# Gating the S5 output by halves of the tokens, and keeping its first half on chip until the output projection

## The chip, the cores and the metric

The kernel runs on one core of a Trainium2 chip. A core has TensorE for matrix products (PE in the profile; PEld is its weight load), VectorE (DVE), ScalarE (ACT), GpSimd (POOL), and SyncE (SP), which here issues nearly all transfers between HBM and the on-chip SBUF. The engines run their own instruction lists in order and wait for each other by semaphores. PSUM is the memory that TensorE writes its results to; it has eight banks of 2 KB per partition.

The metric is the time on the device in microseconds, as the median of several executions. One more execution is recorded by the profiler; the trace is from that one.

## What is computed

One layer of a hybrid decoder with 1024 tokens of width 1024 in float32: an input projection feeds eight RWKV heads (512 channels) and an S5 state-space group (512 channels); what both give is joined, projected by `w_out`, gated and added to the residual; then comes a SwiGLU feed-forward part (FFN). Cut to what matters here:

```python
def rwkv7_time_mix(...):          # sequential in the tokens; done here by chunks
    ...                           # S <- S*w + (S a) b + v k ;  y = S r
    y = (y - mu) * lax.rsqrt(var + LNX_EPS) * lnx_w + lnx_b
    y = y + jnp.sum(r_h * k_h * r_k, axis=-1, keepdims=True) * v_h
    return y.reshape(bsz, seq, D_RWKV) * g

def s5_mix(...):
    ...                           # y: (B, T, 512), out of the state-space recurrence
    zz = jax.nn.gelu(y)
    out = zz * jax.nn.sigmoid(zz @ w_glu + b_glu)
    return rms_norm(out) * gain

ada = c_act @ w_ada[l] + b_ada[l]                 # six vectors of 1024
sh_m, sc_m, g_m, sh_f, sc_f, g_f = jnp.split(ada, 6, axis=-1)
mix = jnp.concatenate([y_rwkv, y_s5], axis=-1) @ w_out[l]
x = x + g_m[:, None, :] * mix
h = modulate(rms_norm(x), sh_f, sc_f)
ffn = (jax.nn.silu(h @ ffn_w_gate[l]) * (h @ ffn_w_up[l])) @ ffn_w_down[l]
x = x + g_f[:, None, :] * ffn
```

## The kernel before

**Products.** A float32 product is three passes with operands split into a rounded part and a remainder: `split(dst, src, eng)` lets ACT cast the rounded part (L131 of the helper) and `eng` subtract it (`lo_part`, L127). So every operand of a split product costs one ACT and one POOL or DVE instruction ahead of TensorE.

**Stages.** After the S5 part, RWKV goes by four quarters of 256 tokens, `qt` 0 to 3. Each has `prepare` and `post` (matrices of the chunks, a triangular solve on DVE in which `XU`, `stmp` and `LU` take part, a trip through DRAM in `x_d`), `chains` (four chunks in sequence, each of four steps with products into `p` and small DVE copies `R`, `U`, `ST` between them) and `finishes` (`finish(q)` for two groups of four heads: norm, gate, `ld` written to `y_d`). Two other strands run beside quarter 1: `s5_glu`, the gate of S5's output, and `ada_steps`, which makes three of the six adaLN vectors (48 loads `wada` of 256 KB, four per step, in four buffers; of twelve steps, half accumulate `acc` wholly on DVE at L297, and half by ACT, L299, and POOL, L300). Then `outproj(0)` projects the first 512 tokens (`po`), and the first half's FFN runs while RWKV's quarters 2 and 3 are woven into it. `outproj(1)` and the second half's FFN end the program.

**s5_glu.** S5's output lies in DRAM (`z_d`) by position within chunks of eight tokens: `z_d[t]` holds position t of all 128 chunks. The GLU takes four units of 256 tokens; unit `hf` is positions 2hf and 2hf+1 of all chunks, so a unit holds tokens of the whole sequence. Per unit: two loads `zz`, a split of it (`zhl`), four products `pglu` of 12 matmuls into the PSUM banks `s` and `p` in turn, `sg`/`zz` (L807, L808), the sum of squares on POOL, one product `pss` into bank `s`, the scale `ra`, `rs` (L819, L820), four scalings of `zz` on DVE (L823) and one write to rows 512 to 1023 of `y_d` (L825).

**outproj(half).** For each half of the output columns (`dh`) it goes over k = 4, 5, 6, 7, 0, 1, 2, 3, eight pieces of 128 rows of `w_out`; k of 4 and above are S5's. Per k it loads `yt` from `y_d` (in the first `dh`), splits it into `yhl`, loads `wraw`, splits that into `wo` (POOL does the remainder), and issues 12 matmuls `po` into four banks. These banks have the tags `s`, `p`, `A` and `G` and are also those of RWKV, the GLU and adaLN. A half has 192 `po` in all.

**What sets the order.** The code is emitted by generators that `weave` interleaves with given weights; then a scheduler with modelled times of its own fixes each engine's instruction list. In the stage of the chains of quarter 0 (`c0`) the call is `weave(c0, (LIM(glg, 18), 2), LIM(adg, 12))`: up to 18 steps of the GLU and 12 of adaLN beside them.

Of the kernel before, what the change touches and what calls it, by code (L numbers as in the profile page):

```python
# [29 lines left out]
def kernel(  # L30
# [745 lines left out]
    def s5_glu(glp):  # L776
# [21 lines left out]
        nxt = load(0)
        for hf in range(4):
            zz, hl = nxt  # L800
            ssum = glp.tile([P, 256], F32, tag="x2", bufs=6, name="ssum")
            for m in range(4):
# [485 lines left out]
    def outproj(half, xp, op, tags, gp, gt):  # L1288
# [18 lines left out]
        for dh in range(2):  # L1307
            sl = slice(HT * dh, HT * dh + HT)
            pss = [ps_t(t, "po") for t in tags]
            for k in order:  # L1310
# [22 lines left out]
    def norm_f(half, xp, tags):  # L1333
# [158 lines left out]
```

## Time and profile before

| what | value |
| --- | --- |
| median of 3 runs | 1584.49 us (1580.01 to 1585.1) |
| the profiled execution | 1576.36 us |
| its span in the trace | 1574.6 us |
| mean granted TensorE clock | 0.937 |
| TensorE busy | 1418.4 us, 90% of the span |
| VectorE, ScalarE, GpSimd busy | 925.9, 574.6 and 553.4 us |

All trace numbers are from the profiled execution, which is 8.1 us faster than the median of the runs. Its time is 1.8 us more than its span. The stretch that the change touches lies between 425 and 725 us: the chains of quarter 0 with GLU and adaLN, the chains and finishes of quarter 1, the first half's output projection and the first FFN block. The granted clock is 1.00 where TensorE runs at the upper of its two levels (2.4 GHz) all the time; at 0.5 it is at 1.2 GHz.

### The profile page before, as it was taken

What the parts mean: (1) busy time and instruction counts of PE and PEld (TensorE: products, weight loads), DVE (VectorE), ACT (ScalarE), POOL (GpSimd) and SP (SyncE); (2) the same over time, 40 slices, a digit from 0 to 9 for tenths busy, and PEclk for the clock granted to TensorE, in tenths of its full rate; (3) what the DMA queues carried; (4) which work ended last, traced back from release to release, by engine and by line L of the source; (5) the groups of instructions that cost most, each with busy time, mean ns of one, the idle gap of its engine ahead of it and who ended that gap; (6) DMA issues with size and microseconds to landing.
All of it is one profiled execution on the core that took longest, in us unless ns stands there. A gap on an engine that the chain in (4) does not pass through costs nothing.

```text
span 1574.6 us, 22988 instructions
## 1 busy us (share of the span) xinstructions
PE 1418.4 (90%) x9071; PEld 1145.1 (73%) x9071; DVE 925.9 (59%) x1591; ACT 574.6 (36%) x924; POOL 553.4 (35%) x499
## 2 busy tenths in 40 slices
PE   3897798898968868898999998999997999999997
PEld 3776586776757647776777786778886888888885
DVE  6977328889687964854478654547347433433335
ACT  4432334554345554242154222224333322222223
POOL 4359435332164425381000026001511254544443
PEclk9889898999889758999999998999998999999999
DMA  9724555353456444254042344216422333232331
GB/s 291 228 97 140 167 173 165 108 153 102 91 160 175 140 132 140 68 128 94 28 121 81 101 101 94 81 55 199 143 74 77 124 101 100 91 97 94 107 94 54
DMA packets 259885, 187.67 MB, mean 119 GB/s; under 512 B 71479, under 2 KB 228801, under 8 KB 259777
## 3 DMA queue, kind: packets, MB, share of 16 engines
q1 hardware_dynamic: 256048, 178.00, 38.5%
q10 hardware_dynamic: 2912, 7.64, 1.4%
q8 instruction: 71, 1.16, 0.3%
q0 software_dynamic: 816, 0.57, 0.2%
q14 instruction: 38, 0.30, 0.1%
HBM read 157.11 MB, written 31.16 MB: 120 GB/s over the span
## 4 chain that ended last, share of the span: by engine, by line
PE 58%; DVE 16%; DMA 8%; POOL 8%; ACT 4%; issue 4%; SPq 1%; ACTq 0%; DVEq 0%; POOLq 0%
PE pdn L270 12%; PE pgate L270 12%; PE pup L270 12%; PE pz L270 6%; PE po L1320 3%; PE p L1065 2%; POOL stmp L1009 2%; POOL XU L1011 2%; DVE acc L297 2%; PE pu L367 2%; PE pY L765 1%; DMA wada<-in_w_ada_dram 1%; DMA XU<-x_d 1%; PE pA L965 1%; DMA raw_g<-in_ffn_w_gate_dram 1%
## 5 line engine op out<-in xcount | busy, mean ns | idle before, releaser
L270 PE MATMUL pdn<-wd,act 128*128 128x512 f32 x1056 | 271.8, 398 | 1.0 <-DVE x L1369 0.8
L270 PE MATMUL pup<-h,hl_up 128*128 128x512 f32 x1056 | 264.9, 394 | 0.2 <-ACT hl_up L131 0.2
L270 PE MATMUL pgate<-h,hl_g 128*128 128x512 f32 x1056 | 262.5, 394 | 2.0 <-ACT hl_g L131 1.9
L270 PEld LDWEIGHTS pdn<-wd,act 128*128 128x128 f32 x1056 | 197.3, 190 | 48.5 <-issue 2.5
L270 PEld LDWEIGHTS pgate<-h,hl_g 128*128 128x128 f32 x1056 | 196.5, 188 | 46.8 <-issue 2.9
L270 PEld LDWEIGHTS pup<-h,hl_up 128*128 128x128 f32 x1056 | 197.1, 188 | 43.8 <-issue 2.1
L1369 DVE TENSOR_TENSOR x<-pdn,x 128x512 f32<-128x512 f32 x176 | 118.8, 687 | 183.7 <-PE pdn L270 183.5
L270 PE MATMUL pz<-hT,hl_z 128*128 128x256 f32 (+1 forms) x912 | 185.8, 361 | 27.3 <-ACT zo L875 8.4
L270 PEld LDWEIGHTS pz<-hT,hl_z 128*128 128x128 f32 x912 | 151.3, 206 | 57.5 <-ACT zo L875 11.8
L1404 DVE TENSOR_TENSOR rawd<-rawd,gfb 128x1024 f32<-128x1024 f32 x44 | 56.9, 1294 | 98.0 <-DMA rawd<-in_ffn_w_down_dram 76.9
L1320 PE MATMUL po<-wo,yhl 128*128 128x512 f32 x384 | 94.7, 398 | 1.4 <-POOL wo L127 0.8
L131 ACT CAST hl_up<-raw_up 128x1024 fp32r<-128x1024 f32 x44 | 46.2, 1051 | 118.7 <-PE pup L270 105.7
L131 ACT CAST wd<-rawd 128x1024 fp32r<-128x1024 f32 x44 | 45.6, 1051 | 118.7 <-DVE rawd L1404 84.6
L1320 PEld LDWEIGHTS po<-wo,yhl 128*128 128x128 f32 x384 | 72.3, 190 | 18.5 <-POOL wo L127 1.7
L127 POOL TENSOR_TENSOR hl_g<-raw_g,hl_g 128x1024 fp32r<-128x1024 f32 x19 | 45.6, 2398 | 80.1 <-ACT hl_g L131 76.1
L127 POOL TENSOR_TENSOR yhl<-yt,yhl 128x512 fp32r<-128x512 f32 x16 | 23.2, 1457 | 143.5 <-ACT yhl L1305 140.1
L1398 ACT ACTIVATE sgt<-pgate 128x512 f32<-128x512 f32 x44 | 26.3, 599 | 120.7 <-PE pgate L270 120.5
L1009 POOL TENSOR_TENSOR stmp<-LU,XU 128x126 f32<-128x126 f32 (+22 forms) x62 | 31.6, 510 | 108.9 <-DMA LU<-l_d 104.2
L127 POOL TENSOR_TENSOR wd<-rawd,wd 128x1024 fp32r<-128x1024 f32 x19 | 49.8, 2619 | 55.4 <-ACT wd L131 55.4
L878 POOL TENSOR_TENSOR zo<-zo,zm 128x512 f32<-128x512 f32 x28 | 43.9, 1568 | 70.3 <-ACT zo L875 58.3
L127 POOL TENSOR_TENSOR wo<-wraw,wo 128x512 fp32r<-128x512 f32 x32 | 43.0, 1350 | 72.8 <-ACT wo L131 72.8
L127 POOL TENSOR_TENSOR hl_up<-raw_up,hl_up 128x1024 fp32r<-128x1024 f32 x19 | 49.7, 2617 | 50.7 <-ACT hl_up L131 50.7
(373 smaller groups left out, 2461.5 us busy)
## 6 DMA issues: line engine op xcount, KB each, us to landing
raw_g<-in_ffn_w_gate_dram SPq DMA_DIRECT2D x44, 512.0 KB, 3.9
raw_up<-in_ffn_w_up_dram SPq DMA_DIRECT2D x44, 512.0 KB, 3.8
rawd<-in_ffn_w_down_dram SPq DMA_DIRECT2D x44, 512.0 KB, 3.3
wada<-in_w_ada_dram SPq DMA_DIRECT2D x24, 512.0 KB, 8.3
raw_z<-in_w_in_dram SPq DMA_DIRECT2D x24, 512.0 KB, 5.5
wada<-in_w_ada_dram SPq DMA_DIRECT2D x48, 256.0 KB, 3.5
wraw<-in_w_out_dram SPq DMA_DIRECT2D x32, 256.0 KB, 3.3
zt_d<-zo SPq DMA_DIRECT2D x28, 256.0 KB, 2.8
```

The lines of the kernel that those rows point to most:

```text
L127: (eng or G).tensor_tensor(out=out, in0=a, in1=b, op=ALU.subtract)
L131: S.copy(dst[:, 0], src)
L270: PE.matmul(ps, lhsT=lf(a, k), rhs=rf(b, k), start=(n == 0), stop=(n == 3 * kb - 1))
L297: V.scalar_tensor_tensor(out=acc, in0=wt, scalar=cact[:, k:k + 1], in1=acc, op0=ALU.mult, op1=ALU.add)
L367: PE.matmul(pu[hf, b], lhsT=uw[b][:, a_, k, :], rhs=hT[hf, k][:, b_, :], start=(k == 0 and n == 0), stop=(k == 7 and n == 2))
L878: G.tensor_tensor(out=o, in0=o, in1=zm[:, 0:HT], op=ALU.add)
L1009: SOLVE.tensor_tensor(out=t, in0=LU[:, j, j + 1:32].unsqueeze(2).to_broadcast([P, nt, nk]), in1=X[:, j:j + 1, 0:nk].to_broadcast([P, nt, n ...
L1011: SOLVE.tensor_tensor(out=X[:, j + 1:32, 0:nk], in0=X[:, j + 1:32, 0:nk], in1=t, op=ALU.add)
L1065: PE.matmul(ps[r, h], lhsT=a, rhs=b, start=(n == 0), stop=(n == len(ops) - 1))
L1320: PE.matmul(pss[i], lhsT=yh[k][:, a, 128 * i:128 * i + 128], rhs=wo[:, b], start=(k == 4 and n == 0), stop=(k == 3 and n == 2))
L1369: V.tensor_tensor(out=t, in0=ps, in1=t, op=ALU.add)
L1404: V.tensor_tensor(out=raw, in0=raw, in1=gfb, op=ALU.mult)
```

## The change

A GLU unit is now four of the eight positions, but only of the first or second 64 chunks: units 0 and 1 hold the first 512 tokens, units 2 and 3 the rest. A load of `zz` is four transfers with runs of 256 bytes in place of two with 512. The first half's y is not written to DRAM. It is split (ACT copy, POOL remainder) straight into `yh[4]` to `yh[7]`, which take the SBUF slots of the first quarter's matrices `ak0` and `ak1`. The second half's y still goes to `y_d`, in eight writes instead of two. `finish` of quarter 1 splits its `ld` on DVE into the second half of `yh[0]` to `yh[3]` and writes no `y_d`; of quarter 0 it writes as before, and `outproj(0)` loads only those 256 tokens.

The weave of the chains of quarter 0 takes four steps of the GLU (the first unit's products) and no more, so the other units come with quarter 1. `wraw` has three buffers, and in half 0 the remainder of `wo` is made by DVE for odd k, by POOL for even k.

```diff
-        def load(hf):
+        def load(u):
             zz = glp.tile([P, 4, 256], F32, tag="zz", bufs=2, name="zz")
-            for t in range(2):
-                nc.sync.dma_start(zz[:, :, 128 * t:128 * t + 128], z_d[2 * hf + t].rearrange("b c g j -> (c g) b j"))
+            half, t0 = u // 2, 4 * (u % 2)
+            for t in range(4):
+                nc.sync.dma_start(zz[:, :, 64 * t:64 * t + 64],
+                                  z_d[t0 + t, :, :, :, 64 * half:64 * half + 64].rearrange("b c g j -> (c g) b j"))
...
+            if u == 0:
+
+                for q in range(2):
+                    t = RP[0].tile([P, 2, 2, HT], F32R, tag=f"ak{q}", name="y5")
+                    for x in range(2):
+                        yh[4 + 2 * q + x] = t[:, x]
             for m in range(4):
                 V.scalar_tensor_tensor(out=zz[:, m], in0=zz[:, m], scalar=hga[:, m:m + 1], in1=rs,
                                        op0=ALU.mult, op1=ALU.mult)
-            nc.sync.dma_start(y_d[512:1024, 256 * hf:256 * hf + 256].rearrange("(m p) t -> p m t", p=P), zz)
+                if half == 0:
+                    v = zz[:, m].rearrange("p (t j) -> p j t", t=4)
+                    d = yh[4 + m].rearrange("p x (j t) -> p x j t", t=8)[:, :, :, t0:t0 + 4]
+                    S.copy(d[:, 0], v)
+                    lo_part(d[:, 1], v, d[:, 0], G)
+                else:
+                    nc.sync.dma_start(
+                        y_d[512 + 128 * m:640 + 128 * m, :].rearrange("p (t j) -> p t j", t=8)[:, t0:t0 + 4, 64:128],
+                        zz[:, m].rearrange("p (t j) -> p t j", t=4))
...
         V.tensor_tensor(out=d, in0=pg, in1=rs, op=ALU.mult)
-        nc.sync.dma_start(y_d[256 * q:256 * q + 256, QT * qt:QT * qt + QT].rearrange("(h p) t -> p h t", h=2),
-                          d.rearrange("p (h t) -> p h t", h=2))
+        if qt == 1:
+            for h in range(2):
+                split(yh[2 * q + h][:, :, QT:HT], d[:, QT * h:QT * h + QT], V)
...
-    weave(c0, (LIM(glg, 18), 2), LIM(adg, 12))
+    weave(c0, LIM(glg, 4), LIM(adg, 12))
...
         def y_load(k):
+            if half == 0 and k >= 4:
+                return
+            n = HT if half else QT
...
-                raw = op.tile([P, HT], F32, tag="wraw", bufs=2, name="wraw")
+                raw = op.tile([P, HT], F32, tag="wraw", bufs=3, name="wraw")
...
-                split(wo, raw, G)
+                split(wo, raw, (V if k % 2 else G) if half == 0 else G)
```

Three places in the engines' lists show how the order moves. Before, SyncE's list behind the last load of quarter 1's solve (`VT<-x_d`) reads as follows; `wada` are the loads of `ada_steps`, `zz<-z_d` those of a GLU unit, `y_d<-zz` the write of one:

```order
L1024 DMA VT<-x_d 64x16x32 x2
L825 DMA y_d<-zz 128x4x256
L285 DMA wada<-in_w_ada_dram 128x2x256
L793 DMA zz<-z_d 128x4x128 x2
L285 DMA wada<-in_w_ada_dram 128x2x256 x7
L825 DMA y_d<-zz 128x4x256
L285 DMA wada<-in_w_ada_dram 128x2x256 x3
L793 DMA zz<-z_d 128x4x128 x2
L285 DMA wada<-in_w_ada_dram 128x2x256 x9
```

And in the changed kernel, from the same load on:

```order
L1040 DMA XU<-x_d 128x16x16 x2
L1041 DMA VT<-x_d 64x16x32 x2
L285 DMA wada<-in_w_ada_dram 128x2x256 x32
L902 DMA kz<-zt_d 128x2x256
L794 DMA zz<-z_d 128x4x64 x4
L1341 DMA wraw<-in_w_out_dram 128x1x512
L902 DMA rz<-zt_d 128x2x256
L1341 DMA wraw<-in_w_out_dram 128x1x512
L1147 DMA y_d<-ld 128x2x256
L1341 DMA wraw<-in_w_out_dram 128x1x512
```

The 32 loads that come here up to the end of adaLN are the same; GLU loads and writes that stood among them are gone from the row or stand behind it.

On TensorE, the end of quarter 1 before: `pd`, `pv`, `pg` are the three products of a `finish`, `pw` and `pa` belong to quarter 2's `prepare`, `pss` to the last GLU unit, and this is where the first `po` stands:

```order
L1102 MATMUL pd<-ar,cen 128x512
L904 MATMUL pw<-wzk,wa_132 128x256 x2
L816 MATMUL pss<-ssum,ones 128x256
L1102 MATMUL pd<-ar,cen 128x512
L904 MATMUL pa<-wzk,wa_132 128x256 x2
L1109 MATMUL pv<-lsq,blk 128x512 x2
L1124 MATMUL pg<-gs,g2w 128x256 x4
L1270 MATMUL pgb<-dgb,ones 128x128 x2
L1320 MATMUL po<-wo,yhl 128x512 x8
```

The same place in the changed kernel, from quarter 2's last `pa` on (18 more `po` stand ahead of these rows; `y_4563` and `y_4564` are the kept S5 rows):

```order
L921 MATMUL pa<-wzk,wa_132 128x256 x2
L1346 MATMUL po<-wo,y_4563 128x512 x6
L1346 MATMUL po<-wo,y_4564 128x512 x3
L1119 MATMUL pd<-ar,cen 128x512
L819 MATMUL pss<-ssum,ones 128x256
L1119 MATMUL pd<-ar,cen 128x512
L1346 MATMUL po<-wo,y_4563 128x512 x6
L1346 MATMUL po<-wo,y_4564 128x512 x3
L1126 MATMUL pv<-lsq,blk 128x512
L1346 MATMUL po<-wo,y_4564 128x512 x12
L1126 MATMUL pv<-lsq,blk 128x512
L1346 MATMUL po<-wo,yhl 128x512 x10
```

60 of the 192 `po` of half 0 now stand ahead of the last `pg`, against none, and 132 behind it.

On VectorE, the rows around the first GLU scaling `ra<-pss` before, right behind the solve's last instruction (`VT<-XU`):

```order
L1074 COPY U<-p_4521 128x128
L1012 COPY VT<-XU 128x32x16
L819 TENSOR_SCALAR ra<-pss 128x256
L1078 TENSOR_TENSOR ST<-p_4588,ST 128x128
L252 TENSOR_TENSOR ra<-ra,rs 128x256
L1079 TENSOR_TENSOR ST<-ST,pc 128x128
L253 SCALAR_TENSOR_TENSOR ra<-ra,rs 128x256
L254 SCALAR_TENSOR_TENSOR rs<-ra,rs 128x256
L823 SCALAR_TENSOR_TENSOR zz<-zz,hga,rs 128x256 x4
```

And the rows around unit 0's `ra<-pss` in the changed kernel, where `acc` are adaLN's accumulations and `lsq`, `lrs` belong to a `finish` of quarter 0:

```order
L307 SCALAR_TENSOR_TENSOR mod<-pac_4522,cols 128x2
L297 SCALAR_TENSOR_TENSOR acc<-wada,cact,acc 128x256
L1091 COPY U<-p_4592 128x128
L252 TENSOR_TENSOR lsq<-lsq,lrs 128x512
L297 SCALAR_TENSOR_TENSOR acc<-wada,cact,acc 128x256
L253 SCALAR_TENSOR_TENSOR lsq<-lsq,lrs 128x512
L297 SCALAR_TENSOR_TENSOR acc<-wada,cact,acc 128x256
L254 SCALAR_TENSOR_TENSOR lrs<-lsq,lrs 128x512
L822 TENSOR_SCALAR ra<-pss 128x256
L1134 SCALAR_TENSOR_TENSOR lrs<-ld,cols,lrs 128x256 x2
L1135 SCALAR_TENSOR_TENSOR lrs<-lrs,cols,bo 128x256
```

All of adaLN's accumulations on VectorE now stand ahead of the first GLU scaling; before, the first three GLU scalings stood among them.

## Rows read from the trace of the kernel before

**Rows 1.** The windows view, by the stages of this stretch (us from the span's start): chains of quarter 0 with the solve of quarter 1; chains of quarter 1; finishes of quarter 1; output projection of half 0; first FFN preparation. Busy time (instructions) of each engine, granted clock, DMA share, GB/s.

```profile
core 0: us, PE busy (x) PEld busy (x) DVE busy (x) ACT busy (x) POOL busy (x), PEclk, DMA share, GB/s
425.00:476.60 51.60, 38.56 (x545) 33.23 (x546) 41.77 (x110) 24.73 (x60) 27.52 (x38) 0.74 0.55 150
476.60:567.50 90.90, 74.59 (x989) 61.97 (x987) 75.33 (x175) 45.48 (x96) 37.19 (x43) 0.80 0.55 161
567.50:595.00 27.50, 16.21 (x32) 7.28 (x32) 17.82 (x36) 16.70 (x27) 3.76 (x3) 0.62 0.49 152
595.00:646.00 51.00, 49.37 (x210) 39.15 (x210) 25.47 (x34) 19.72 (x33) 28.87 (x22) 0.96 0.32 98
646.00:674.30 28.30, 22.13 (x221) 17.86 (x219) 24.02 (x46) 11.30 (x23) 9.46 (x6) 1.00 0.35 82
```

**Rows 2.** The chain of waits that ends last, through 500 to 597 us: start us, duration us, what.

```profile
503.89 3.89 DMA wada<-in_w_ada_dram
508.58 3.26 DMA wada<-in_w_ada_dram
...
548.23 2.71 DMA wada<-in_w_ada_dram
...
582.33 1.68 DVE zz L823 x4
584.02 3.25 DMA y_d<-zz
587.29 7.23 DMA yt<-y_d
594.56 1.10 issue
595.70 1.54 POOL yhl L127
```

**Rows 3.** The timeline: the last instruction of `finish(1)` of quarter 1, the end of half 0's last `po` and what TensorE does next (start us, duration us).

```profile
594.20 0.69 DVE L1125 TENSOR_TENSOR ld<-pg,lrs 128x512 f32<-128x512 f32 x1
...
641.74 5.10 PE L1320 MATMUL po<-wo,yhl 128*128 128x512 f32 x20
646.77 0.44 PE L965 MATMUL pA<-ar,bk 64*64 64x128 f32 x4
```

**Rows 4.** The chain of waits again, inside `outproj(0)`: 36 `po` in a row without a gap.

```profile
632.96 8.46 PE po L1320 x36
```

**Rows 5.** Groups by line and shape from 435 to 600 us: count, busy us, mean ns of one, idle time before them and what ended it.

```profile
L300 POOL TENSOR_TENSOR acc<-acc,wada 128x256 f32<-128x256 f32 x42 | 34.1, 812 | 24.2 <-DVE U L1074 11.0 <-PE pn L924 5.5 <-ACT wada L299 5.5
...
L297 DVE SCALAR_TENSOR_TENSOR acc<-wada,cact,acc 128x256 f32<-128x256 f32 x42 | 22.8, 544 | 0.2
...
L823 DVE SCALAR_TENSOR_TENSOR zz<-zz,hga,rs 128x256 f32<-128x256 f32 x16 | 8.6, 598 | 0.1
...
L808 DVE SCALAR_TENSOR_TENSOR zz<-sg,zz 128x256 f32<-128x256 f32 x16 | 8.3, 516 | 5.7 <-ACT sg L807 5.7
...
L1078 DVE TENSOR_TENSOR ST<-p,ST 128x128 f32<-128x128 f32 x16 | 4.5, 283 | 0.3
...
L127 POOL TENSOR_TENSOR wo<-wraw,wo 128x512 fp32r<-128x512 f32 x3 | 3.8, 1268 | 17.6 <-ACT wo L131 17.6
...
L1125 DVE TENSOR_TENSOR ld<-pg,lrs 128x512 f32<-128x512 f32 x4 | 2.7, 682 | 0.1
...
L1305 ACT CAST yhl<-yt 128x512 fp32r<-128x512 f32 x2 | 2.1, 1079 | 0.2 <-DMA yt<-y_d 0.2
...
L1140 DVE TENSOR_SCALAR gs<-gs 128x256 f32<-128x256 f32 x2 | 0.9, 450 | 0.0
```

**Rows 6.** The groups of the tile `act`, VectorE's line of them: remainders of 128x512 made by VectorE (min, median, max ns).

```profile
L127 DVE TENSOR_TENSOR act<-sgt,act x44: 678/787/1706, 688.9 to 1553.0; 128x512 fp32r<-128x512 f32 x44
```

**Rows 7.** The timeline of SyncE's queue: issue runs of `wada` loads (duration is that of the whole run), and the loads of `VT`.

```profile
436.03 2.04 SPq L285 DMA_DIRECT2D wada<-in_w_ada_dram  x4
...
480.58 1.87 SPq L1024 DMA_DIRECT2D VT<-x_d  x2
...
488.34 13.39 SPq L285 DMA_DIRECT2D wada<-in_w_ada_dram  x7
...
508.58 18.54 SPq L285 DMA_DIRECT2D wada<-in_w_ada_dram  x9
...
545.72 12.00 SPq L285 DMA_DIRECT2D wada<-in_w_ada_dram  x7
```

**Rows 8.** The view of transfers, groups of two tiles: KB each, median us from issue to landing.

```profile
wada<-in_w_ada_dram SPq DMA_DIRECT2D x48, 256.0 KB, 3.5
...
zz<-z_d SPq DMA_DIRECT2D x8, 256.0 KB, 3.1
```

**Rows 9.** The groups of the tile `wada` from 425 to 575 us: `acc` at L295 (min, median, max ns).

```profile
L295 DVE TENSOR_SCALAR acc<-wada,cact x12: 336/353/2456, 441.7 to 555.6; 128x256 f32<-128x256 f32 x12
```

**Rows 10.** The timeline around the longest of those, both of its neighbours on POOL and DVE (start us, duration us).

```profile
448.91 2.41 POOL L127 TENSOR_TENSOR zhl<-zz,zhl 128x1024 fp32r<-128x1024 f32 x1
449.01 2.46 DVE L295 TENSOR_SCALAR acc<-wada,cact 128x256 f32<-128x256 f32 x1
```

**Rows 11.** The timeline behind the projection: quarter 2's `LU` loads on SyncE, the first FFN product, and the first solve product of quarter 2 with its wait in brackets.

```profile
671.20 1.79 SPq L1001 DMA_DIRECT2D LU<-l_d  x2
...
674.27 0.96 PE L270 MATMUL pgate<-h,hl_g 128*128 128x512 f32 x3
...
720.53 1.92 PE L1031 MATMUL pG<-XU,ak 32*32 32x32 f32 x64 [4.59 <-DMA XU<-x_d]
```

More of the change, by code (lines that the diff above doesn't have):

```diff
@@ L798, in s5_glu @@
         nxt = load(0)
-        for hf in range(4):
+        for u in range(4):
+            half, t0 = u // 2, 4 * (u % 2)
             zz, hl = nxt
@@ L811, in s5_glu @@
                     G.tensor_tensor(out=ssum, in0=ssum, in1=sg, op=ALU.add)
-                if m == 2 and hf < 3:
-                    nxt = load(hf + 1)
+                if m == 2 and u < 3:
+                    nxt = load(u + 1)
                 yield
@@ L1125, in finish @@
         V.tensor_tensor(out=d, in0=pg, in1=rs, op=ALU.mult)
-        nc.sync.dma_start(y_d[256 * q:256 * q + 256, QT * qt:QT * qt + QT].rearrange("(h p) t -> p h t", h=2),
-                          d.rearrange("p (h t) -> p h t", h=2))
+        if qt == 1:
+            for h in range(2):
+                split(yh[2 * q + h][:, :, QT:HT], d[:, QT * h:QT * h + QT], V)
+        else:
+            nc.sync.dma_start(y_d[256 * q:256 * q + 256, QT * qt:QT * qt + QT].rearrange("(h p) t -> p h t", h=2),
+                              d.rearrange("p (h t) -> p h t", h=2))
         yield
     lora = {}
+    x1, yh, h2 = {}, {}, {}
     def lora_in(qt):
@@ L1272, in bcast_gate @@
         return t
-    x1, yh, h2 = {}, {}, {}
     sq2 = [ssq, tcol]
@@ L1293, in y_load @@
         def y_load(k):
-            yt = op.tile([P, HT], F32, tag="yt", bufs=2, name="yt")
-            hl = yh[k] = xp.tile([P, 2, HT], F32R, tag=f"yh{k}", name="yhl")
+            if half == 0 and k >= 4:
+                return
+            n = HT if half else QT
+            yt = op.tile([P, HT], F32, tag="yt", bufs=2, name="yt")[:, 0:n]
+            if half or k >= 4:
+                yh[k] = xp.tile([P, 2, HT], F32R, tag=f"yh{k}", name="yhl")
+            hl = yh[k][:, :, 0:n]
             src = y_d[128 * k:128 * k + 128, :]
             if k < 4:
-                nc.sync.dma_start(yt, src[:, HT * half:HT * half + HT])
+                nc.sync.dma_start(yt, src[:, HT * half:HT * half + n])
                 split(hl, yt, G)
@@ L1337, in norm_f @@
         pl, ta, tb = (op, "wraw", "yt") if half else (fp, "raw", "ftmp")
-        dgt = pl.tile([P, HT if half else D], F32, tag=ta, bufs=2, name="dg")
+        dgt = pl.tile([P, HT if half else D], F32, tag=ta, bufs=3 if half else 2, name="dg")
         dgs = [dgt[:, 128 * i:128 * i + 128] for i in range(4)]
@@ L1426 @@
     xp0 = pool("xp0", stack=xs0)
+    for k in range(4):
+        yh[k] = xp0.tile([P, 2, HT], F32R, tag=f"yh{k}", name="yhl")
     late = seq(*[g for qt in (2, 3) for g in (prepare(qt), post(qt), chains(qt), finishes(qt))])
```

## Prediction

> **What bounds the kernel now.** I read the windows view first, by stages [rows 1]. Between 476.6 and 567.5 us TensorE is busy 74.59 of 90.9 us and DVE 75.33; neither is full, and the granted clock is 0.80, so TensorE is at its lower level for part of it. Between 567.5 and 595, where quarter 1's `finish` runs, TensorE is busy 16.21 of 27.5 us at 0.62. Then comes the output projection, with TensorE busy 49.37 of 51 us at 0.96. The reader is to see a half-empty stage in front of a full one. The chain of waits [rows 2] says what holds the full one back: the last GLU unit's scaling at 582.33, its write to `y_d` of 3.25 us, the load `yt` of 7.23 us, and POOL's split `yhl` until 597.24. Earlier the same chain goes through `wada` loads. At the same time as the load, `finish(1)` of quarter 1 ends: call F the end of its last `ld`, 594.20 + 0.69 = 594.9 [rows 3]. The last `po` of half 0 ends at 646.8 [rows 3], 51.9 us behind F.
>
> **The projection moved ahead of F.** 36 `po` take 8.46 us when nothing stops them [rows 4], 0.235 us each, so 192 take 45.1 of the 51.9 us and 6.8 are the start, small products and waits. In the changed order 60 `po` stand ahead of the last `pg` and 132 behind. Before F TensorE has 27.5 - 16.2 = 11.3 us idle in the finishes alone [rows 1], and more in the chains. If all 60 fit, the distance from F to the end of the projection falls by 60 x 0.235 = 14.1 us. Nothing else of the change shortens what lies behind F by as much: the S5 rows' trip through DRAM (3.25 + 7.23 us [rows 2]) lies ahead of 597 and ends 1.2 us after `finish(1)` does, so cutting it alone would give about that, inside the 6.8. POOL loses eight `yhl` splits there, but TensorE is the full engine. So the first term is **-14.1**.
>
> **F moves later: DVE's work.** Up to F, DVE gets more to do. Counted from the solve's last copy `VT` to the last `ld` in the two orders, and priced with the groups [rows 5, 6]: two more L808 (2 x 0.52), six small chain instructions of quarter 0 that now come later (6 x 0.283), three remainders of `wo` (3 x 0.68, the shortest of DVE's 128x512 remainders), two of `finish`'s new splits at half that size (2 x 0.4, an estimate from half of 0.68 and a start cost) and one L1140 (0.45), together 6.0 us. DVE was busy 75.33 + 17.82 = 93.2 of 118.4 us there, 0.787 [rows 1]. If its share of waiting stays, F moves by 6.0 / 0.787 = 7.6 us. The other end of this term is 0, if all of it fills gaps.
>
> **F moves later: the row of 32 loads.** The second count does not rest on the first. On SyncE, 32 `wada` loads now follow the load of `VT` in one row; GLU loads and writes stood among them. On DVE all of adaLN's `acc` stand ahead of unit 0's `ra`, and all of the GLU's scalings, both finishes of quarter 0, the rest of quarter 1's chains and its finishes are queued behind them: 59 us of DVE work by the same durations. Unit 0 waits for it, then its `zz` buffer, then unit 2's load. So F = A + 59 / density, with A the time of the last `acc`. The row begins at 480.58 + 1.87 = 482.45 [rows 7]. A buffer's round is an issue of 2.04 / 4 = 0.51 [rows 7], 3.5 to land [rows 8], and either two L297 on DVE, 2 x 0.544, or one ACT step and two POOL additions, about 0.5 + 2 x 0.812 [rows 5]: 5.1 or 6.1 us, over four buffers 1.27 or 1.53 us per load. Half of the steps are of each kind: 1.40. Then A = 482.45 + 32 x 1.40 + 3.5 + 1.1 = 531.9, and at the density of the chains' stage, 75.33 / 90.9 = 0.829 [rows 1], F = 531.9 + 71.2 = 603.1, a slip of 8.2. Both counts agree on 8, and I take **+8**. The nearest rows bound it from both sides: unblocked issue, 0.51 per load, would leave DVE's own work as the limit (7.6 or less); the runs of `wada` that stand among other work took 13.39 / 7 = 1.91, 18.54 / 9 = 2.06 and 12.00 / 7 = 1.71 [rows 7]. I take the round because in the changed order nothing foreign stands in the row on SyncE, and those three runs each had a GLU or finish step that the buffers waited for. They are the far end: at 2.06, A = 553, F = 624.2, a slip of 29.
>
> **Smaller parts.** The `zz` loads double in number with half the run length; unit 1's load is one unit ahead of use, so I cost it at nothing, with unit 0's products as the cover; unit 2's comes behind the row of loads and before `wraw`, and four issues at 0.5 us more are 1 us if that cover is gone. A load of `zz` took 3.1 us to land [rows 8]; double that would still be before its use. The eight ACT copies and POOL remainders of the kept rows are on engines that were busy 45.48 and 37.19 of 90.9 us [rows 1]: nothing, or up to 2 us for the one that releases the first `po`. `wraw`'s third buffer: a load earlier, nothing. Sharing `wo`: POOL takes 1.27 for one [rows 5] and TensorE needs 12 x 0.235 = 2.8 us for a k, so POOL was not late by its own time; nothing gained. Behind the projection, quarter 2's first product waits 4.59 us for its solve [rows 11]; in the changed order two FFN loads stand ahead of its `LU` on SyncE and 18 more FFN matmuls ahead of it on TensorE. I take zero, with an end of +4 (the 1.79 us of `LU` and two loads ahead) if the solve, not TensorE, ends last.
>
> Sum: -14.1 + 8 = **-6.1**, and the profiled execution of 1576.4 would go to 1570. That execution lies 8.1 under the median; taking the same difference off the median gives 1584.5 - 6 = **1578.5 us**.
>
> **A rule weighed.** The trace has one `acc` at L295 that took 2.46 us against a median of 0.353 [rows 9]; it began at 449.01 and ended with POOL's `zhl`, 448.91 + 2.41 [rows 10]. The Trainium skill, page "SBUF — State Buffer", section "SBUF: two separate sides", says that VectorE and GpSimd share a port pair as an exclusive lock, so that a VectorE instruction with two SBUF inputs waits for the whole of a GpSimd one that reads SBUF. By that rule, which these rows bear out, handing every other `wo` remainder to DVE buys DVE the wait for the POOL one beside it: up to 3 x 1.35 = 4 us ahead of F, and the sum would be -2, no change that can be told. By the density of DVE, which has such waits in it already, it stays at -6.
>
> **The rivals.** (a) **F does not slip.** DVE's new work fills its gaps (25 us of 118 idle [rows 1]) and the loads run at their round. Then the full 14.1 is kept: 1570.4; with some of the 6.8 us of start gone too, 1567. For it: DVE is not full. Against: a fifth idle is what a chain of dependent small copies leaves anyway.
>
> (b) **The slip eats the gain.** At 1.6 us per load A = 538.3, F = 609.5, slip 14.6: +0.5. The same comes if DVE waits for POOL in the splits, or if the projection ends 6 us earlier and the solve of quarter 2 is late by 4. 1584. For it: the range of paces seen; against: the round above.
>
> (c) **The row of loads sets the time, and it is slower.** The place is SyncE's row of 32 `wada` with all of the GLU's first-half scalings behind its last `acc` on DVE. The price is 32 times the excess of the pace. It decides from a slip of 14.1 + 4.75 = 18.9 us, that is F above 613.8, A above 542.6, a pace above 1.73 us per load. Two of the three runs seen are above that, the third just below [rows 7]. At 1.91, A = 548.2, F = 619.4, slip 24.5: +10, 1594.9. Against: those three were mixed with other work, whose waits are in them.
>
> (d) **The change does not do what it says:** the 60 `po` are issued, but wait. `po` need banks `s` and `p`, which GLU unit 3's products and `pss` still use, and `wo`, whose split waits for ACT and then POOL or DVE; `pd` and `pv` of `finish(1)` are queued behind them on TensorE. Then the 14.1 is not won and the 8 is lost: 1592. Against: the first 18 `po` are in banks `A` and `G` alone.
>
> **How the numbers follow.** 0.3% of the time, 4.75 us, is about what a measurement of this kernel can tell from no change. Chances: the forecast 0.35, (a) 0.12, (b) 0.28, (c) 0.17, (d) 0.08. Faster by more than 0.3% are the forecast and (a), 0.47; within it (b), 0.28; slower (c) and (d), 0.25. The likeliest single case is the forecast, whose own range is the two counts of the slip, 5 to 9 us: 1575 to 1580. The range that is to hold 8 in 10 begins at (a)'s far end, 1567, and ends at (c) with a pace of 1.9, 1595; cut out are paces near 2.06 and a faster end behind the projection.
>
> **What would show it.** Right: in the windows of the finishes TensorE busy rises by about 14 us and the granted clock with it; from the last `ld` to the last `po` 38 us in place of 51.9; the last `ld` at about 603; a row of 32 `wada` at 1.4 us each, the last `acc` near 532; the first `po` reads `y_4563` and no `yt` load stands in the chain of waits. Wrong: a last `acc` above 543 (c); `po` with idle time ahead of them, released by `wo` or a GLU step (d); a wait at quarter 2's first `pG` of 8 us or more (b). The whole argument rests on F; if `finish(1)` ends at 595 as before, it is (a).

## The result, and the profile after

The changed kernel takes 1599.47 us in the median of 6 runs (1588.15 to 1602.05), the kernel before 1584.85 on the same chip: a ratio of 1.0101, interval 1.0072 to 1.0131. It is slower by 1%, 11 to 21 us, and lies above the predicted range. Its profiled execution took 1591.45 us (span 1589.7), 15.1 more than that of before.

The windows view after, by the stages that answer to [rows 1]: chains of quarter 0; the row of `wada` loads up to the last `acc`; from there to the end of the last `ld`; the rest of the projection; up to the first FFN product. Columns as there.

```profile
425.00:476.60 51.60, 37.10 (x422) 31.68 (x421) 42.95 (x109) 22.65 (x58) 25.94 (x38) 0.60 0.57 152
476.60:532.20 55.60, 44.04 (x519) 34.94 (x519) 29.14 (x77) 20.53 (x46) 21.50 (x32) 0.59 0.60 166
532.20:620.30 88.10, 75.30 (x635) 57.98 (x634) 68.36 (x136) 48.72 (x92) 27.69 (x26) 0.87 0.36 104
620.30:653.30 33.00, 32.18 (x146) 26.08 (x145) 24.79 (x40) 12.38 (x25) 7.24 (x7) 1.00 0.19 59
653.30:681.80 28.50, 21.98 (x215) 18.18 (x213) 23.21 (x44) 10.98 (x21) 8.99 (x6) 0.94 0.25 63
```

Where before had two mixed stages (DVE busy 0.83 and 0.65 of the time), there is now a thin one and a thick one. For 55.6 us DVE is busy 29.14 and the granted clock is 0.59; the 88.1 us behind it hold what was left. The timeline after, line by line: the row of loads, adaLN's last `acc`, the four GLU scalings, the last `ld`, the end of half 0's `po`, the first FFN product and quarter 2's first solve product.

```profile
480.87 45.70 SPq L285 DMA_DIRECT2D wada<-in_w_ada_dram  x32
...
531.70 0.48 DVE L297 SCALAR_TENSOR_TENSOR acc<-wada,cact,acc 128x256 f32<-128x256 f32 x1
...
532.70 0.42 DVE L822 TENSOR_SCALAR ra<-pss 128x256 f32<-128x256 f32 x1
...
561.64 0.42 DVE L822 TENSOR_SCALAR ra<-pss 128x256 f32<-128x256 f32 x1 [0.46 <-PE pss L819]
...
583.48 0.42 DVE L822 TENSOR_SCALAR ra<-pss 128x256 f32<-128x256 f32 x1
...
600.21 0.42 DVE L822 TENSOR_SCALAR ra<-pss 128x256 f32<-128x256 f32 x1 [1.81 <-PE pss L819]
...
619.58 0.69 DVE L1142 TENSOR_TENSOR ld<-pg,lrs 128x512 f32<-128x512 f32 x1
...
642.30 11.05 PE L1346 MATMUL po<-wo,yhl 128*128 128x512 f32 x48
...
681.84 4.62 PE L270 MATMUL pgate<-h,hl_g 128*128 128x512 f32 x19 [0.74 <-DVE ftmp L1375]
...
734.69 1.92 PE L1048 MATMUL pG<-XU,ak 32*32 32x32 f32 x64 [6.40 <-DMA XU<-x_d]
```

The row takes 45.70 us for 32 loads, 1.43 each, and the last `acc` ends at 532.2: both as forecast. But the scalings follow at 532.7, 561.6, 583.5 and 600.2, and the last `ld` ends at 620.3, not 603. From there to the end of the last `po` (642.30 + 11.05 = 653.35) it is 33.0 us in place of 51.9 [rows 3].

The sum, against the trace of before: last `ld` +25.4, from it to the last `po` -18.9, from that to the first FFN product +1.0 (28.5 for 27.5), from the first FFN product to the end +7.6 (907.9 for 900.3). Together +15.1.

### The profile page after: what moved, and what is told of

Read it like the earlier page. It is cut to its first block, busy times and chain, and to the rows that moved or that the text cites. A ratio compares the mean times of both kernels' runs of the same rounds, so it can differ in the third digit from the quotient of the medians.

```text
span 1589.7 us, 23027 instructions
## 1 busy us (share of the span) xinstructions
PE 1433.2 (90%) x9071; PEld 1157.6 (73%) x9071; DVE 941.4 (59%) x1603; ACT 567.9 (36%) x928; POOL 536.9 (34%) x495
## 4 chain that ended last, share of the span: by engine, by line
PE 45%; POOL 4%; DMA 4%; DVE 4%; ACT 2%; issue 1%; SPq 0%; DVEq 0%; ACTq 0%; POOLq 0%
PE pdn L270 13%; PE pgate L270 13%; PE pup L270 13%; PE p L1082 2%; PE po L1346 2%; POOL XU L1028 2%; POOL stmp L1026 2%; DMA LU<-l_d 1%; PE ptr L1372 1%; PE pA L982 1%; DMA raw_up<-in_ffn_w_up_dram 1%; DMA XU<-x_d 1%; DMA raw_g<-in_ffn_w_gate_dram 1%; DVE yo L1354 0%; DMA y_d<-ld 0%
## 5 line engine op out<-in xcount | busy, mean ns | idle before, releaser
L270 PEld LDWEIGHTS pz<-hT,hl_z 128*128 128x128 f32 x912 | 152.8, 209 | 55.6 <-ACT zo L892 10.4
L1430 DVE TENSOR_TENSOR rawd<-rawd,gfb 128x1024 f32<-128x1024 f32 x44 | 56.9, 1293 | 86.0 <-DMA rawd<-in_ffn_w_down_dram 60.2
L131 ACT CAST wd<-rawd 128x1024 fp32r<-128x1024 f32 x44 | 45.5, 1048 | 109.0 <-DVE rawd L1430 83.3
L1346 PE MATMUL po<-wo,yhl 128*128 128x512 f32 x288 | 72.0, 402 | 0.7 <-POOL wo L127 0.7
L127 POOL TENSOR_TENSOR wd<-rawd,wd 128x1024 fp32r<-128x1024 f32 x19 | 49.7, 2617 | 55.6 <-ACT wd L131 55.6
L895 POOL TENSOR_TENSOR zo<-zo,zm 128x512 f32<-128x512 f32 x28 | 43.9, 1569 | 71.2 <-ACT zo L892 59.1
L297 DVE SCALAR_TENSOR_TENSOR acc<-wada,cact,acc 128x512 f32<-128x512 f32 (+1 forms) x84 | 61.1, 734 | 7.5 <-DMA wada<-in_w_ada_dram 6.5
L1346 PEld LDWEIGHTS po<-wo,yhl 128*128 128x128 f32 x288 | 54.6, 192 | 13.0 <-POOL wo L127 1.4
L131 ACT CAST hl_g<-raw_g 128x1024 fp32r<-128x1024 f32 x44 | 45.9, 1044 | 48.9 <-DMA raw_g<-in_ffn_w_gate_dram 48.9
```

The source lines that it names most:

```text
L127: (eng or G).tensor_tensor(out=out, in0=a, in1=b, op=ALU.subtract)
L131: S.copy(dst[:, 0], src)
L270: PE.matmul(ps, lhsT=lf(a, k), rhs=rf(b, k), start=(n == 0), stop=(n == 3 * kb - 1))
L297: V.scalar_tensor_tensor(out=acc, in0=wt, scalar=cact[:, k:k + 1], in1=acc, op0=ALU.mult, op1=ALU.add)
L895: G.tensor_tensor(out=o, in0=o, in1=zm[:, 0:HT], op=ALU.add)
L1346: PE.matmul(pss[i], lhsT=yh[k][:, a, 128 * i:128 * i + 128], rhs=wo[:, b], start=(k == 4 and n == 0), stop=(k == 3 and n == 2))
```

## Experiments

Three theories. **Order**: the weave emits all of adaLN ahead of the GLU's first scaling, so one row of loads leaves the engines thin and everything else queues behind. **Handling**: keeping y on chip (copies, remainders, short runs, shared splits) costs more than it saves. **Clock**: the thin stretch drops TensorE to its lower level, and that is the loss. The table gives, from each trace, the `po` ahead of the last `pg`, the end of the last `ld` and of half 0's last `po`, the time from the first FFN product to the end, and the ratio of run times to before with its 95% interval.

| kernel | po ahead | last ld | last po | FFN to end | ratio [interval] |
| --- | --- | --- | --- | --- | --- |
| before | 0 | 594.9 | 646.8 | 900.3 | 1 |
| before, second trace (e9) | 0 | 594.7 | 648.4 | 901.3 | |
| changed | 60 | 620.3 | 653.3 | 907.9 | 1.0101 [1.0072, 1.0131] |
| changed again (e10) | 60 | 621.1 | 654.1 | 908.4 | 1.0111 [1.0089, 1.0134] |
| e1 weave only | 0 | 612.7 | 666.6 | 905.3 | 1.0185 [1.0146, 1.0223] |
| e2 second half first | 48 | 606.4 | 643.0 | 907.5 | 1.0019 [0.9997, 1.0041] |
| e3 more matmuls | 48 | 612.0 | 651.2 | 907.2 | 1.0079 [1.0055, 1.0104] |
| e4 adaLN spread | 66 | 622.2 | 652.0 | 907.6 | 1.0039 [1.0009, 1.0068] |
| e5 e2, FFN slower | 48 | 598.3 | 635.0 | 918.7 | 1.0079 [1.0051, 1.0107] |
| e6 splits on POOL | 60 | 620.2 | 655.9 | 905.4 | 1.0082 [1.0052, 1.0112] |
| e7 before, FFN slower | 0 | 591.8 | 645.3 | 915.4 | 1.0093 [1.0059, 1.0128] |
| e8 e2 and matmuls | 66 | 615.4 | 646.9 | 907.4 | 1.0033 [1.0011, 1.0054] |
| e11 eight buffers | 66 | 624.0 | 656.6 | 905.2 | 1.0016 [1.0002, 1.0031] |
| e12 e2, eight buffers | 62 | 613.0 | 644.1 | 902.3 | 1.0001 [0.9983, 1.0018] |

Three traces are shifted from before 425 us on. The load `XU` of quarter 0's solve is issued at 417.5 us in the changed kernel and at 419.5 before, but at 421.9 in e4, 414.0 in e5 and 428.1 in e11, so the ends of these three are not read against the others' by themselves. From the last `po` to the end of the program it is 927.8 and 928.8 us in the two traces of before, 943.0 in e7, 946.9 in e5, and 933 to 937 in all the others.

**e1, the weave alone.**

```diff
 # in the kernel before
-    weave(c0, (LIM(glg, 18), 2), LIM(adg, 12))
+    weave(c0, LIM(glg, 4), LIM(adg, 12))
```

> The kernel before with one line of the change: the weave of quarter 0's chains takes four GLU steps and all of adaLN. GLU units, y_d and the projection are those of before, and no po stands ahead of the last pg. Order theory (what costs is that all of the GLU after its first products is queued behind one row of wada loads): the last ld of finish(1) moves from 595 to 612 to 620, nothing is won, and the time is 1600 to 1610. Handling theory (what costs is keeping y on chip: copies, remainders, short runs, shared splits): no change, 1581 to 1589. Clock theory (the stretch beside the row is so thin on TensorE that it runs at its lower level): as the order theory, with a granted clock of at most 0.65 between 480 and 530.

Measured: 1.0185, 29 us slower (23 to 35), nearly twice the loss of the whole change, with nothing kept on chip. The first line is the kernel before; then e1's windows from 480 us, and the GLU scalings and the last `ld` in its timeline:

```profile
480.00:530.00 50.00, 41.76 (x570) 34.36 (x572) 37.63 (x87) 29.75 (x61) 21.44 (x25) 0.86 0.60 165
...
480.00:530.00 50.00, 32.08 (x406) 24.77 (x402) 25.25 (x65) 19.57 (x44) 20.85 (x31) 0.58 0.63 175
530.00:612.70 82.70, 63.12 (x580) 46.07 (x580) 63.09 (x132) 44.10 (x80) 16.58 (x15) 0.78 0.36 111
...
529.30 0.42 DVE L819 TENSOR_SCALAR ra<-pss 128x256 f32<-128x256 f32 x1
...
557.24 0.42 DVE L819 TENSOR_SCALAR ra<-pss 128x256 f32<-128x256 f32 x1 [0.79 <-PE pss L816]
...
580.40 0.42 DVE L819 TENSOR_SCALAR ra<-pss 128x256 f32<-128x256 f32 x1 [1.03 <-PE pss L816]
...
592.96 0.40 DVE L819 TENSOR_SCALAR ra<-pss 128x256 f32<-128x256 f32 x1
...
611.97 0.69 DVE L1125 TENSOR_TENSOR ld<-pg,lrs 128x512 f32<-128x512 f32 x1
```

The scalings (529, 557, 580, 593) come 3 to 7 us ahead of those of the changed kernel, all behind the last `acc` as there. The row behind `VT` is 25 loads here, and the load of `VT` itself ends 6 us later than before. DVE is busy 25.25 us from 480 to 530; in the kernel before it was 37.63 in the same window. Those 12 us are done later. The handling theory falls as the cause of the loss: the weave alone costs all of it and more, and beside this weave the rest of the change wins back 1.0185 - 1.0101, some 13 us. The clock is 0.58 here, as the clock theory wants too.

**e2, the second half's units first**, so that 14 GLU steps can stand beside quarter 0's chains again:

```diff
 # in the changed kernel
-        nxt = load(0)
-        for u in range(4):
+        nxt = load(2)
+        for u in (2, 3, 0, 1):
...
-                if m == 2 and u < 3:
-                    nxt = load(u + 1)
+                if m == 2 and u != 1:
+                    nxt = load((u + 1) % 4)
...
-    weave(c0, LIM(glg, 4), LIM(adg, 12))
+    weave(c0, (LIM(glg, 14), 2), LIM(adg, 12))
```

> The changed kernel with the GLU's units in the order 2, 3, 0, 1, so that 14 GLU steps (two units that go to y_d whole, and the first unit of the kept half up to its products) can again stand beside quarter 0's chains at weight 2, as in the kernel before. All that is kept on chip is as in the change; 48 po stand ahead of the last pg. Order theory: the last ld at 595 to 605, 1572 to 1585, faster than the changed kernel by 15 to 25. Handling theory: the slip stays, last ld at 612 or later, 1592 to 1602. Clock theory: granted clock above 0.75 between 425 and 530 and the time of the order theory.

Measured: 1.0019; half 0's last `po` ends at 643.0, 10 earlier than in the changed kernel and 4 earlier than before. The last `ld` (606.4) missed the order theory's 605 by a little. Yet the time is no better than before: behind the first FFN product it takes 907.5 us in place of 900.3, as the changed kernel does. The granted clock rose here as well (0.65 from 425 to 480 us, 0.88 from 480 to 530), so this run alone does not part order from clock.

**e3, matmuls whose result nothing reads**, to lift the clock and leave the order of the loads and of DVE (48 of them; 48 `po` instead of 60 stand ahead of the last `pg`, so TensorE's order is not quite the same):

```diff
 # in the changed kernel, ada_cols, after the column products
+        if n == 2:
+            for _ in range(4):
+                PE.matmul(wide[:, 128:384], lhsT=ones, rhs=acc, start=True, stop=True)
...
```

> The changed kernel with four matmuls of 128x256 whose result nothing reads after each adaLN column product (48 in all, some 25 us of TensorE at the upper level) in a stretch where TensorE is busy 0.79 of the time at its lower level. The order of loads and of DVE stays. Clock theory: granted clock 0.85 or more between 440 and 555, the last ld before 612, 1585 to 1593, faster than the changed kernel although TensorE does more. Order theory: the clock may rise, but the row of 32 wada still takes 45 us and the last ld stays at 616 to 626; 1597 to 1606.

The changed kernel's windows, then e3's:

```profile
480.00:530.00 50.00, 38.44 (x461) 30.45 (x461) 23.77 (x64) 20.00 (x44) 21.23 (x31) 0.60 0.62 177
530.00:560.00 30.00, 25.06 (x224) 19.85 (x224) 22.85 (x49) 15.02 (x29) 11.76 (x10) 0.69 0.38 107
...
480.00:530.00 50.00, 44.66 (x577) 35.18 (x575) 28.75 (x71) 20.87 (x46) 21.22 (x31) 0.90 0.58 175
530.00:560.00 30.00, 26.12 (x272) 20.74 (x270) 22.72 (x49) 15.46 (x32) 12.36 (x10) 0.89 0.43 111
```

The clock is 0.90 and 0.89, where the changed kernel had 0.60 and 0.69. The last `ld` ends at 612.0, the last `po` at 651.2, 2 earlier, and the ratio is 1.0079, an interval that overlaps that of the changed kernel. Between the two forecasts: the clock with these matmuls may be worth some us, not the 15. What the matmuls cost by themselves is inside this figure.

**e4, adaLN spread over both chains.**

```diff
 # in the changed kernel
-    weave(c0, LIM(glg, 4), LIM(adg, 12))
+    weave(c0, LIM(glg, 4), LIM(adg, 5))
...
-    weave(LIM(c1, 14), finishes(0), (glg, 1), (adg, 3))
+    weave(LIM(c1, 14), finishes(0), (glg, 2), (adg, 1))
```

> The changed kernel with two weave numbers: five adaLN steps beside quarter 0's chains in place of twelve, and beside quarter 1's chains two GLU steps to one of adaLN in place of one to three. The wada loads stand in runs of 17, 5, 1, 1, 3, 2, 3 with the GLU's loads between them in place of one row of 32; unit order and all that is kept are the change's; 66 po stand ahead of the last pg. Order theory: the last ld at 600 to 610, 1580 to 1590. Handling theory: 1595 to 1602. Clock theory: depends on the clock alone: if it stays at 0.6 until 530, the time stays at 1595 or above.

Measured: 1.0039, better by 10 us, though the last `ld` did not come earlier (622.2; 66 `po` stand ahead of it, and the last `acc` now ends at 578) and the last `po` only by 1 in its trace. But this trace is one of the shifted ones: counted from quarter 0's `XU` load, the last `po` ends after 230.1 us in place of 235.8, 5.7 earlier. The ratio is as the order theory wants; its mark, a last `ld` at 600 to 610, is not, and the last `ld` is no measure by itself where more `po` stand ahead of it.

**e6, all remainders of `wo` on POOL**, two buffers of `wraw`:

```diff
 # in the changed kernel
-                raw = op.tile([P, HT], F32, tag="wraw", bufs=3, name="wraw")
+                raw = op.tile([P, HT], F32, tag="wraw", bufs=2 if half == 0 else 3, name="wraw")
...
-                split(wo, raw, (V if k % 2 else G) if half == 0 else G)
+                split(wo, raw, G)
```

> The changed kernel with all remainders of wo on POOL and two buffers of wraw in half 0, as before. It tells two things. Ahead of F: if DVE's splits wait for POOL and cost (the rule weighed in the prediction), the last ld comes 2 to 5 us earlier than the 620 of the changed kernel; if not, it stays at 617 to 622. Behind the projection: this edit alone brings the order back to that of the kernel before (165, 1022 and 1398 FFN matmuls ahead of quarter 2's and quarter 3's first solve product and of half 1's first po; the changed kernel has 180, 1138 and 1536). If the 7 us behind the first FFN product come from that order, that stretch falls to 900 to 902 us and the time lies 7 under the changed kernel's, at a ratio to before of 1.003 to 1.007; if they come from something else, the ratio stays at 1.009 to 1.012.

Measured: the last `ld` at 620.2, as with the shared splits, so these cost nothing ahead of it. Behind the first FFN product 905.4 and not 900 to 902, and that mostly because the product itself comes later: from the last `po` to the end it is 935.9 us, as in the changed kernel (936.4). The order of before does not bring the 7 us back by itself. At 1.0082 the ratio can't tell 1.003 to 1.007 from 1.009 to 1.012.

**e5 and e7, the FFN's share beside quarters 2 and 3.**

```diff
 # e5: in the kernel of e2; e7: in the kernel before
-    alongside(late, f0, 2)
+    alongside(late, f0, 3)
```

> The kernel of e2 (units 2, 3, 0, 1) with one more number changed: three steps of quarters 2 and 3 to one of the first half's FFN in place of two. In the order, 1244 FFN matmuls then stand ahead of half 1's first po, against 1536 in the changed kernel and in e1 to e4, and 1398 before. In those kernels the stretch from the first FFN product to the end takes 905 to 908 us, against 900 before. If that loss of 7 us comes from the first half's FFN having run out when half 1's projection needs cover, this kernel wins it back: 900 us or less there, 1571 to 1576 with before at 1578. If not, it stays within 2 us of e2.

> The kernel before with e5's number alone, three to one: what that number is worth by itself. 1248 FFN matmuls ahead of half 1's first po in place of 1398. If a larger rest of the first half's FFN helps in half 1's projection, 1572 to 1577 against before's 1578; if before's 1398 are enough, within 2 us.

Both missed: 918.7 and 915.4 us behind the first FFN product, 11 and 15 more than without the edit. A larger rest of FFN for half 1's projection is worse, so the idea that the FFN runs out too early finds no support.

**e8, e2 with e3's matmuls.**

> The kernel of e2 with e3's 48 matmuls whose result nothing reads. In e2 the granted clock was 0.65 between 425 and 480 us and 0.67 to 0.70 between 530 and 595, and the last ld ended at 606. Clock theory: the clock goes to 0.85 or more there, the last ld to 598 or earlier, and the time 5 to 8 us under e2. Order theory: the clock may rise, but the last ld stays at 604 to 608 and the time within 3 us of e2.

The granted clock rose to 1.00 (480 to 530), 0.89 (530 to 560) and 0.92 (560 to 595), from 0.88, 0.67 and 0.70 in e2, and the time stayed: 1.0033 for 1.0019. The last `ld` is later, but behind 66 `po` for 48. What these matmuls cost and what the clock gives are not separated, but the 5 to 8 us that the clock theory forecast are not there.

**e9 and e10, the two kernels again.**

> The kernel before, unchanged, for a second trace of it. In the first, the stretch from the first FFN product to the end took 900.3 us; in the changed kernel and in e1 to e4, e6 and e8, one trace each, 905 to 908. If the loss behind the projection is real, 899 to 902 again; if one trace's scatter is as large as that, 904 or more. The last ld at 592 to 598 and half 0's last po at 644 to 650 either way.

> The changed kernel, unchanged, timed beside the next two on one chip and with a second trace. The last ld at 617 to 624, half 0's last po at 650 to 657, and 905 to 909 from the first FFN product to the end, if the first trace stands for it; the ratio to before 1.007 to 1.013.

All as the first traces: 901.3 behind the first FFN product before, 908.4 in the changed kernel. The 7 us are there in both pairs of traces. Two views of the changed kernel's second trace and one of before's show what differs: SyncE's queue around the first FFN product (at 675.9 before, 682.5 changed), and TensorE's waits for `hl_up` behind it. Before:

```profile
672.79 1.76 SPq L1001 DMA_DIRECT2D LU<-l_d  x2
674.60 1.59 SPq L259 DMA_DIRECT2D raw_g<-in_ffn_w_gate_dram  x1
676.28 0.84 SPq L259 DMA_DIRECT2D raw_up<-in_ffn_w_up_dram  x1
```

Changed:

```profile
681.75 0.37 SPq L259 DMA_DIRECT2D raw_g<-in_ffn_w_gate_dram  x1
682.17 0.57 SPq L259 DMA_DIRECT2D raw_up<-in_ffn_w_up_dram  x1
682.91 4.36 SPq L1018 DMA_DIRECT2D LU<-l_d  x2
...
PE pup L270 <- ACT hl_up L131: 3.9, 3, 2.1
```

Before, quarter 2's `LU` was issued 3.1 us ahead of the first FFN product; now two FFN loads stand ahead of it and it is issued 0.4 behind it, and takes 4.36 to issue. Quarter 2's first solve product then comes 53 us after the first FFN product, 46 before, and TensorE waits 3.9 us for `hl_up`, against 0.2 in the first trace of before. That wait is not the cause: e2 has 0.2 us of it too and loses as much. The place can be narrowed. From the last `po` to quarter 2's first solve product it is 73.7 and 73.6 us in the two traces of before, 81.3 and 81.7 in the changed kernel and 80.5 to 81.5 in e1 to e4, e8, e11 and e12; from that product to the end it is 854 to 855 in both kernels. So the loss is whole when quarter 2's solve ends, and the weave alone (e1) brings it too. Which step of quarter 2's preparation it starts from stays open.

**e11, eight buffers for the loads, in the changed kernel; e12, the same in e2.**

```diff
-                todo.append((ada_acc(pl, ada_load(pl, part, j, 2, 4), 2, V if mix(j) else None), part, j))
+                todo.append((ada_acc(pl, ada_load(pl, part, j, 2, 8), 2, V if mix(j) else None), part, j))
```

> The changed kernel with eight buffers for wada in place of four: 23 loads stand behind the load of VT instead of 32, and the row no longer waits four loads behind its use. Weave, unit order and what is kept stay; 66 po stand ahead of the last pg. Order theory: the row ends 8 to 14 us earlier (last acc at 518 to 524 in place of 532), the GLU behind it starts that much earlier, half 0's last po comes at 642 to 648, and the ratio is 1.000 to 1.005. If instead the work behind the row sets the time, whatever the row does, the last po stays at 650 to 655 and the ratio at 1.007 to 1.012.

> Both remedies: units 2, 3, 0, 1 beside quarter 0's chains as in e2, and eight buffers for wada. Its order behind the projection is that of the kernel before (166, 1022 and 1398 FFN matmuls ahead of the same three points), and 62 po stand ahead of the last pg. Order theory: half 0's last po at 634 to 640, and with 900 to 905 us from the first FFN product the time is 5 to 12 us under before, a ratio of 0.992 to 0.997. If eight buffers only move waits to other places, 0.999 to 1.004 as in e2.

e11 is at 1.0016 beside 1.0111 for the changed kernel on the same chip: one number, in a line of adaLN that the change did not touch, wins back 13 us by the medians, 15 by the ratios. Its trace is the late one (the profiled execution is the slowest of its 13; up to the `XU` load the granted clock was 0.89, in the changed kernel 0.92), so its rows are read from the end of the `VT` load, and its windows are those of the changed kernel moved by as much, 14.5 us:

```profile
493.74 1.57 SPq L1041 DMA_DIRECT2D VT<-x_d  x1
495.36 20.76 SPq L285 DMA_DIRECT2D wada<-in_w_ada_dram  x23
...
494.50:544.50 50.00, 35.56 (x485) 28.66 (x482) 31.31 (x77) 23.48 (x47) 25.37 (x31) 0.64 0.55 159
544.50:624.00 79.50, 68.19 (x582) 50.42 (x581) 55.41 (x121) 47.68 (x88) 19.03 (x21) 0.91 0.33 96
```

The row of 23 takes 20.76 us, 0.90 per load; the last `acc` ends 28 us after the load of `VT` (523.7; 51 in the changed kernel), the last `po` 161.3 after it (172.5). DVE is busy 31.31 us of 50, where it was 23.77. The clock there is 0.64 for 0.60, hardly higher, while the loss of run time is gone. With e3 and e8, where a higher clock won little or nothing, the clock theory falls as the main cause. Of the 23 us by which the row ends earlier, 11 arrive at the last `po`; the work behind it takes the rest. Part of that lead was paid ahead of it: nine of the loads now stand before the `VT` load, which comes 4 us later behind the `XU` load, so counted from there the last `po` is 7 us earlier.

e12 ties with before (1.0001) and with e2 (1.0019): in a kernel without the one row, eight buffers win nothing that can be told. That speaks for the row as what they repair in e11. Eight buffers in the kernel before were not tried. The last `po` of e12 ends at 644.1, not 634 to 640, and from there to the first FFN product it takes 33 us in place of 27.5 to 28.5. No kernel tried beats the one before.

## Why the prediction was wrong

**The step that failed** is "Both counts agree on 8, and I take **+8**": the last `ld` moved by 25.4. It is the term for the row of loads that was too small. The second count, F = A + 59 / density, had A right (pace 1.40 for 1.43, last `acc` 531.9 for 532.2). The stretch behind it was forecast at 71.2 us and took 88.1. DVE was busy 68.36 us in it, for 59, and at a density of 0.776, for 0.829: 11.3 of the missing 16.9 us are work that was not counted, 5.6 the density.

**The work left out.** The list behind the 59 us names the GLU's scalings, the finishes and the rest of the chains, but not quarter 2's `prepare`, which stands ahead of the last `ld` in both kernels. 25 of its DVE instructions fall into this stretch, 18.8 us by their durations; those of all the others add up to 56.9, near the 59. (Consecutive instructions overlap a little, so that 75.7 us of durations are 68.36 of busy time.) The four costliest of `prepare`'s groups there, and below them e1's window of the same stretch:

```profile
L958 DVE SCALAR_TENSOR_TENSOR bk<-kn,th 128x512 f32<-128x512 f32 x1 | 2.7, 2745 | 0.0
L926 DVE TENSOR_TENSOR_SCAN th<-m,th 128x512 f32<-128x512 f32 x2 | 2.4, 1224 | 0.1
L953 DVE TENSOR_TENSOR ar<-rz,Pt 128x512 f32<-128x512 f32 x2 | 1.4, 682 | 0.0
L949 DVE SCALAR_TENSOR_TENSOR kn<-kz,nkk,kn 128x256 f32<-128x256 f32 x2 | 1.3, 674 | 0.0
...
529.40:612.70 83.30, 63.26 (x580) 46.23 (x580) 63.69 (x133) 44.35 (x80) 16.58 (x15) 0.78 0.35 110
```

With it the second count gives 531.9 + 68.36 / 0.829 = 614.4, a slip of 19.5 and a sum of +5.4. So the agreement of the two counts on 8 was chance.

**The density.** In e1 it is 63.69 / 83.3 = 0.765. 0.829 was that of a stage in which chains, GLU and adaLN stood beside each other; behind the row adaLN is gone. That they filled each other's waits is an argument, not a measurement.

**What e1 adds.** With the weave alone the last `ld` is late by 612.7 - 594.9 = 17.8; the rest of the change adds the other 7.6. Of these, 2.8 are a later last `acc` and 4.8 the stretch behind it, in which DVE is busy 68.36 us for 63.69. That is near the first count's 6.0 us of new DVE work, but the 7.6 also holds the 60 `po` that `finish` now queues behind on TensorE, so the agreement is not a proof of the term.

**Rival (c)** named the place (all of the GLU's scalings behind the last `acc`) and the sign, and its +10 was near the measured +15. Its condition was wrong: it was to decide from a pace of 1.73 per load, but at 1.43 it had decided already, so that nearness is luck. Rival (a) and the forecast needed a last `ld` at 603 or earlier, (b) in its first form one at 609.5, and (d) that the projection behind it did not get shorter; it got 18.9 us shorter.

**The first term, -14.1,** was too small for what it named: 51.9 fell to 33.0, by 18.9. 14.1 are the 60 `po`; of the 6.8 us of start and waits, 33.0 - 132 x 0.235 = 2.0 are left. That the S5 rows' load and split were the other 5 is likely, but not shown by itself.

**Behind the projection** the forecast took zero, with an end of +4 "if the solve, not TensorE, ends last". It was +7.6, and 7.1 in the second pair of traces: half of the measured +15.1. The solve does end last (quarter 2's first solve product waits 6.40 us for `XU`, 4.59 before), and the loss is whole by then; what delays it is open.

**The rule weighed** asked for up to 4 us of DVE's waits in the splits. e6 shows none at the last `ld`. The row it was read from [rows 9, 10] is a `tensor_scalar` with one tensor input, so it shows an instruction held beside POOL's, but not the case of two inputs that the splits are. That case is in the trace of the changed kernel, in one of the three splits ahead of the last `ld`, and once more in `prepare` (timeline):

```profile
549.03 1.79 POOL L127 TENSOR_TENSOR wo<-wraw,wo 128x512 fp32r<-128x512 f32 x1
...
550.02 1.36 DVE L127 TENSOR_TENSOR wo<-wraw,wo 128x512 fp32r<-128x512 f32 x1
...
577.52 2.64 POOL L127 TENSOR_TENSOR zhl<-zz,zhl 128x1024 fp32r<-128x1024 f32 x1
...
577.97 2.75 DVE L958 SCALAR_TENSOR_TENSOR bk<-kn,th 128x512 f32<-128x512 f32 x1
```

DVE's split began within POOL's and ended 0.56 us after it (551.38 for 550.82), 1.36 us long where the other two took 0.68. `bk` ended 0.56 us after POOL's `zhl` as well (580.72 for 580.16), 2.75 us long where it took 0.68 in e1. Both pairs agree with the Trainium skill, page "SBUF — State Buffer", section "SBUF: two separate sides", by which a VectorE instruction with two SBUF inputs that comes second to a GpSimd one reading SBUF is blocked for the whole of it. In the splits the wait was 0.7 us, once; that of `bk` was 2.1 us and no part of the forecast.

## What to carry over

Two counts of a delay that agree in size do not check each other: here one had left out 18.8 us of work. A count of what is queued ahead of a point is to be made from the engine's list, every strand in it, not from the strands that the change moves. A density taken from a stage of several strands need not hold once one of them is moved out. Where a change comes with a new interleaving, put the interleaving alone on the chip first: here it cost 29 us by itself, and where GLU steps stand beside quarter 0's chains again (e2, e12) the rest of the change ties with the kernel before.

## What the runs showed of the hardware

A row of 32 loads of 256 KB with four buffers was issued at 1.43 us per load; a row of 23 with eight, in a kernel whose source differs in nothing else, at 0.90. TensorE's granted clock was no guide to the time. Over the 50 us behind 480 it was 0.60 in a kernel at 1.0101 of before and 1.00 in one at 1.0033; over the same stretch of e11 (494.5 to 544.5) it was 0.64, in a kernel at 1.0016. Two VectorE instructions with two SBUF inputs that began within one of GpSimd ended 0.56 us after it: 1.36 us for 0.68, and 2.75 for 0.68.
